# The first stage of a sparse-attention layer: norm, transposes and first projection in pairs of token tiles

## The chip, the cores and the metric

One Trainium2 chip, one of its cores. The metric is the device time of one execution of the whole program in microseconds (us); the kernel before ran three times, 481.62, 481.62 and 482.15 us, median 481.62.

The core's engines are named as in the profile: PE multiplies matrices into eight PSUM banks (PEld loads its weights), ACT is the scalar engine, DVE the vector engine, POOL the general engine; SP issues most DMA transfers. Each engine takes its instructions in the order in which they stand in its queue.

## The reference, cut to what matters

One layer of native sparse attention: x is 512 tokens x 1024, w_in has 5680 columns.

```
u = x * rsqrt(mean(x*x, -1) + 1e-6) * pre_norm_gain
q, kv, g, z = split(u @ w_in, [1024, 6*256, 48, 3072])
k_c, v_c, k_s, v_s, k_w, v_w = split(kv, 6)          # 4 groups x 64 each
kc = silu(blocks(k_c + k_pos) @ k_w1) @ k_w2          # 31 blocks of 32 tokens
vc = silu(blocks(v_c + v_pos) @ v_w1) @ v_w2
o  = three softmax branches (compressed, selected, window), each with a relative bias
y  = sum(sigmoid(g) * o * silu(z)) @ w_out
out = x + rms_norm(y) * post_norm_gain
```

## The kernel before

Every product is made of float32 numbers cut into a high part (a cast to fp32r) and a low part (what the cast left out), as three products, high*high, low*high and high*low, summed in one PSUM bank. The split of weights costs one cast and one subtraction for each piece of 128x1024 (four k-slices of 128 rows by 256 columns): even pieces go to ACT and POOL, odd pieces to DVE alone (L234 to L238). Weights come in through three raw buffers `wr`, split ones lie in three buffers `wh`/`wl`.

The first stage (L258 to L364) makes u transposed, that is `uh` and `ul` (high and low part, 1024 rows on partitions, 512 tokens across), and the first product from it, k_c (`p_kc`, two banks). Four token tiles `xs[t]` of 128x1024 come by DMA. `rms(t)` squares and sums one tile on ACT (L304) and raises the mean to -1/2 on POOL (L86, L90). `prep(t)` scales half a tile by the tokens' factor and by the norm weights, which two PE products with a row of ones had spread over 128 partitions in PSUM (L285 to L295, L314), transposes four 128x128 blocks into one PSUM bank (L319), and cuts the bank in two pieces of 128x256 into `uh` (ACT, L325) and `ul` (DVE, L326). The products k_c run over halves of 256 tokens (`hh`), k-slices, and two column halves (L354 to L362), with the transposes of tiles 2 and 3 in between. `tables()` (L328), written between the two halves, turns the bias table into two tensors with 20 PE products, most of 16 columns, reads them out on DVE, and writes them to DRAM, from where the softmax loads them back.

The second stage (L366 on) adds the position vectors to k_c (`blocks`, eight DVE additions of 64x496, L405), splits the sum into `bh`/`bl` (ACT, DVE and POOL, L414 and L415), makes v_c in the same way (`half_t(2,0)` and `half_t(3,1)`, 48 products of 512 columns, L245 to L247), then v, the MLPs over the blocks (L423 to L425), and so on. From there on the kernel keeps PE fed by a plan that the change doesn't touch.

The order of instructions on an engine comes from a scheduler that reorders what is written, within its own estimates; an instruction named in `keep_in_program_order` stays where it is written among its like. A tile pool that closes (a1, L258) gives its memory to the next one (a2): the first instruction that writes a tile of a2 waits for the last reader of what lay there.

Of the kernel before, what the change touches and what calls it, by code (L numbers as in the profile page):

```python
# [20 lines left out]
D = 1024  # L21
H = 16
DH = 64
G = 4
# [27 lines left out]
def nsa_layer(ctx: ExitStack, tc: tile.TileContext, x, pre_gain, post_gain, table, w_in, w_out,  # L52
# [204 lines left out]

    with tc.tile_pool(name="a1", bufs=1) as a1:  # L258
        grow = a1.tile([1, D], F32, name="grow")
        A.dma_start(grow, pre_gain)  # L260
        warm = a1.tile([1, 1], F32, name="warm")
        A.activation(warm, nhalf[0:1], AF.Tanh)
        one = a1.tile([1, 128], F32, name="one")
        V.memset(one, 1.0)
        ones = a1.tile([1, 128], F32R, name="ones")
        V.tensor_copy(ones, one)
        xs = []
        for t in range(NT):
            xt = a1.tile([128, D], F32, name="xt", bufs=4)
            SP.dma_start(xt, x[t * 128:(t + 1) * 128, :])  # L270
            xs.append(xt)
            if t == 1:
                load_ahead(1)
# [11 lines left out]
        gain = []  # L285
        gh = a1.tile([1, D], F32R, name="gh")
        gl = a1.tile([1, D], F32R, name="gl")
        for i in range(2):
            hs = slice(i * 512, (i + 1) * 512)
            V.tensor_copy(gh[:, hs], grow[:, hs])  # L290
            V.tensor_tensor(gl[:, hs], grow[:, hs], gh[:, hs].bitcast(F32), op=ALU.subtract)
            p = sb()
            T.matmul(p, ones, gh[:, hs], start=True, stop=False)
            T.matmul(p, ones, gl[:, hs], start=False, stop=True)
            gain.append(p)  # L295
        sq = a1.tile([128, D], F32, name="sq")
        banks = [tb, ob, tb]
        nb_ = 0

        rs_ = {}  # L300

        def rms(t):
            ss = a1.tile([128, 1], F32, name="ss", bufs=4)
            tc.keep_in_program_order(A.activation(sq, xs[t], AF.Square, scale=1.0 / 32, accum_out=ss))  # L304
            r = a1.tile([128, 1], F32, name="r", bufs=4)
            rstd(r, ss)
            rs_[t] = r

        def prep(t):
            nonlocal nb_  # L310
            r = rs_[t]
            for kq in range(2):
                hs = slice(kq * 512, (kq + 1) * 512)
                V.scalar_tensor_tensor(xs[t][:, hs], xs[t][:, hs], r, gain[kq], op0=ALU.mult, op1=ALU.mult)  # L314
                p = banks[nb_ % 3]()
                nb_ += 1
                for j in range(4):
                    k = kq * 4 + j
                    T.transpose(p[:, j * 128:(j + 1) * 128], xs[t][:, k * 128:(k + 1) * 128], ident)  # L319
                for jj in range(2):  # L320
                    i = kq * 2 + jj
# [650 lines left out]
```

## Time and profile before

| | |
|---|---|
| median of three runs | 481.62 us |
| the profiled execution | 481.59 us |
| its span (first to last instruction) | 479.80 us |
| PE / PEld / DVE / ACT / POOL busy | 95 / 78 / 68 / 57 / 37 % |
| first k_c product begins | 10.46 us |
| k_c done, v_c begins | 31.89 us |
| v_c done, v begins | 42.72 us |
| first softmax instruction on DVE begins | 116.9 us |

The span is what the trace shows; the 1.79 us between it and the execution's time lie around it. A row of the timeline gives start, length, engine, line and operands (out<-in), and in brackets the idle time of the engine before it with the instruction that ended it. Matmuls are pipelined: the length of one is longer than the distance to the next, and the distance is the cost.

### The profile page before, as it was taken

The numbers are of one execution on the slowest core, as the hardware profiler recorded it, in microseconds if no ns is written. First come the engines' busy times: TensorE is split into PE (matmuls) and PEld (weight loads), VectorE is DVE, ScalarE is ACT, GpSimd is POOL, SyncE is SP. The second block draws the span as 40 slices with busy tenths as digits, with TensorE's granted clock in tenths as the row PEclk, the third lists the DMA queues.
The fourth block names the chain that finished last, engine by engine and source line by source line (L and its number), as shares of the span: only waits on it lengthen the run. The fifth ranks groups of instructions, "written<-read, shape, count | busy, mean of one in ns | idle before, by whom it ended". The sixth has DMA issues, their size and how long they took to land.

```text
span 479.8 us, 6876 instructions
## 1 busy us (share of the span) xinstructions
PE 455.1 (95%) x2330; PEld 375.7 (78%) x2330; DVE 325.8 (68%) x788; ACT 273.6 (57%) x643; POOL 178.7 (37%) x139
## 2 busy tenths in 40 slices
PE   5999999999999989999999999998989999999993
PEld 3898788878888768878888778887768788877872
DVE  6779843844556898675689765668977456775486
ACT  5612232635647758765577865566677456657542
POOL 3324433334134253342243533423434325155153
PEclk9989999999999999999999999999999999999998
DMA  8498375461131231420221323213142121113104
GB/s 288 138 85 271 96 212 138 127 176 45 44 89 44 66 84 50 132 87 8 82 67 44 101 76 89 49 40 109 46 135 84 46 87 45 44 48 119 57 22 154
DMA packets 45501, 44.63 MB, mean 93 GB/s; under 512 B 7751, under 2 KB 38471, under 8 KB 45466
## 3 DMA queue, kind: packets, MB, share of 16 engines
q1 hardware_dynamic: 44424, 44.00, 32.4%
q8 instruction: 18, 0.29, 0.3%
q10 hardware_dynamic: 1042, 0.20, 0.2%
q14 instruction: 17, 0.14, 0.1%
HBM read 41.99 MB, written 2.20 MB: 92 GB/s over the span
## 4 chain that ended last, share of the span: by engine, by line
PE 79%; DVE 8%; ACT 7%; issue 2%; DMA 1%; POOL 1%; SPq 0%; DVEq 0%; ACTq 0%
PE ps_pj L146 9%; PE ps_pj L144 9%; PE ps_pj L145 9%; PE ps_s L589 7%; PE ps_t L683 6%; PE ps_o L692 4%; PE ps_o L691 3%; ACT p L602 2%; PE ps_pj L804 2%; PE ps_s L245 2%; PE ps_pj L806 2%; PE ps_pj L805 2%; PE ps_s L246 2%; PE ps_s L247 2%; PE ps_pj L246 2%
## 5 line engine op out<-in xcount | busy, mean ns | idle before, releaser
L116 POOL TENSOR_TENSOR wl<-wr,wh 128x1024 fp32r<-128x1024 f32 x47 | 113.7, 2418 | 160.7 <-ACT wh L113 146.0
L144 PE MATMUL ps_pj<-uh,wh 128*128 128x512 f32 x240 | 99.4, 414 | 0.0
L145 PE MATMUL ps_pj<-uh,wl 128*128 128x512 f32 x240 | 94.4, 393 | 0.0
L146 PE MATMUL ps_pj<-ul,wh 128*128 128x512 f32 x240 | 94.3, 393 | 0.0
L602 ACT ACTIVATE p<-p,nm 128x512 f32<-128x512 f32 (+3 forms) x128 | 71.7, 561 | 35.5 <-DVE nm L601 34.9
L113 ACT CAST wh<-wr 128x1024 fp32r<-128x1024 f32 x47 | 49.2, 1047 | 40.9 <-DMA wr<-in_nsa_w_in_dram 14.7
L687 DVE TENSOR_TENSOR ptl<-ps_t,pth 128x512 fp32r<-128x512 f32 x80 | 54.7, 686 | 22.5 <-ACT pth L686 21.9
L589 PE MATMUL ps_s<-kd,q 128*128 128x512 f32 (+5 forms) x256 | 62.2, 330 | 0.2 <-DVE zs L675 0.2
L686 ACT CAST pth<-ps_t 128x512 fp32r<-128x512 f32 x80 | 45.9, 578 | 21.7 <-PE ps_t L683 20.8
L146 PEld LDWEIGHTS ps_pj<-ul,wh 128*128 128x128 f32 x240 | 45.1, 188 | 9.9
L589 PEld LDWEIGHTS ps_s<-kd,q 128*128 128x128 f32 x256 | 45.2, 188 | 9.3 <-DVE zs L675 0.5
L601 DVE CUSTOM_DVE_ANT_0 p<-ps_s,bias 128x128 f32<-128x128 f32 (+3 forms) x80 | 34.7, 447 | 23.1 <-PE ps_s L589 22.6
L145 PEld LDWEIGHTS ps_pj<-uh,wl 128*128 128x128 f32 x240 | 45.3, 189 | 5.8
L144 PEld LDWEIGHTS ps_pj<-uh,wh 128*128 128x128 f32 x240 | 45.2, 188 | 5.3
L683 PE MATMUL ps_t<-ident,p 128*128 128x128 f32 x320 | 48.7, 272 | 0.0
L683 PEld LDWEIGHTS ps_t<-ident,p 128*128 128x128 f32 x320 | 39.1, 140 | 6.3
L691 PE MATMUL ps_o<-pth,vt 128*128 128x512 f32 x80 | 32.7, 409 | 2.7 <-ACT pth L686 1.4
L692 PE MATMUL ps_o<-ptl,vt 128*128 128x512 f32 x80 | 32.5, 407 | 0.8 <-DVE ptl L687 0.8
L703 POOL TENSOR_TENSOR y<-otmp,zs 128x256 f32<-128x256 f32 x16 | 11.8, 737 | 47.1 <-DVE otmp L700 47.0
L705 POOL TENSOR_TENSOR otmp<-otmp,zs 128x256 f32<-128x256 f32 x15 | 11.2, 748 | 45.9 <-DVE otmp L700 45.9
L699 DVE TENSOR_TENSOR otmp<-ps_o,otmp 64x256 f32<-64x256 f32 x32 | 13.2, 414 | 21.8 <-ACT otmp L698 21.3
L601 DVE CUSTOM_DVE_ANT_1 p<-ps_s,bias 128x256 f32<-128x256 f32 (+2 forms) x48 | 26.0, 550 | 2.1 <-PE ps_s L589 1.8
(260 smaller groups left out, 897.1 us busy)
## 6 DMA issues: line engine op xcount, KB each, us to landing
wr<-in_nsa_w_in_dram SPq DMA_DIRECT2D x36, 512.0 KB, 3.6
wr<-in_nsa_w_in_dram SPq DMA_DIRECT2D x16, 256.0 KB, 4.3
bias<-toepd SPq DMA_DIRECT2D x16, 256.0 KB, 6.5
wr<-in_nsa_w_out_dram SPq DMA_DIRECT2D x8, 512.0 KB, 4.6
xt<-in_x_dram SPq DMA_DIRECT2D x4, 512.0 KB, 4.1
wr<-in_nsa_cmp_k_w_dram SPq DMA_DIRECT2D x4, 512.0 KB, 4.9
wr<-in_nsa_cmp_v_w_dram SPq DMA_DIRECT2D x4, 512.0 KB, 3.7
xr<-in_x_dram SPq DMA_DIRECT2D x8, 256.0 KB, 2.8
```

Of the source, the lines that this page charges most:

```text
L113: A.copy(h[:, 0:kn], raw[:, 0:kn])
L116: el.tensor_tensor(l[:, 0:kn], raw[:, 0:kn], h[:, 0:kn].bitcast(F32), op=ALU.subtract)
L144: T.matmul(p, a, rh, start=k == 0, stop=False)
L145: T.matmul(p, b, rh, start=False, stop=False)
L146: T.matmul(p, a, rl, start=False, stop=k == KT - 1)
L589: T.matmul(po, qs[h][:, qt * 128:(qt + 1) * 128], kds[h // R][:, i, c0:c0 + n], start=i == 0, stop=i == 1)
L601: V.tensor_tensor_reduce(pd, src, bi, 1.0, BIG, ALU.add, ALU.min, st["nm"][:, hh:hh + 1])
L602: A.activation(po, po, AF.Exp, bias=st["nm"][:, hh:hh + 1], scale=-1.0, accum_out=st["rs"][:, hh:hh + 1])
L683: T.transpose(tp[:, hh * 128:(hh + 1) * 128], st["p"][hh][:, c:c + 128], ident)
L687: V.tensor_tensor(pl, tp, ph.bitcast(F32), op=ALU.subtract)
L691: T.matmul(acc, v, prev[1], start=j == 1, stop=False)
L692: T.matmul(acc, v, prev[2], start=False, stop=j == qt + 1)
```

## The change

Parts, in the order of the program:

- **Norm weights.** They are loaded as 8 rows of 128, transposed once on PE and copied to a [128, 8] tile (L316 to L318 of the changed kernel), so that one column holds the weights of a k-slice on partitions. The scaling by them moves behind the transpose: ACT multiplies while it casts `uh`, DVE multiplies and subtracts in one instruction for `ul`. What is left in front of the transpose is the tokens' factor alone, SBUF to SBUF (`norm`).
- **Squares.** Half of each tile's sum of squares is made on ACT, half on DVE (`rms`).
- **Pairs.** `prep(pair, k)` transposes the blocks of one k-slice of two token tiles into a bank of its own (two transposes, 256 columns used), five banks in turn.
- **Weights.** The two pieces of k_c's weights are split in eight parts of 128x256, all by ACT and POOL (`piece`); the third piece is requested before the small loads.
- **Order.** All this is written down instruction by instruction with `O`, which keeps it in program order; `after()` makes what follows be issued after it. k_c runs pair by pair, k-slice by k-slice.
- **Tables.** `tables()` and the position vectors move behind the first half of v_c; the eight additions of k_c stay in front of them. The splits of `blk` move into the second pool.

```diff
-        for i in range(2):
-            V.tensor_copy(gh[:, hs], grow[:, hs])
-            V.tensor_tensor(gl[:, hs], grow[:, hs], gh[:, hs].bitcast(F32), op=ALU.subtract)
-            T.matmul(p, ones, gh[:, hs], start=True, stop=False)
-            T.matmul(p, ones, gl[:, hs], start=False, stop=True)
...
+        p = sb()
+        O(T.transpose(p[:, :KT], grow, ident[:KT, :KT]))
+        gain = a1.tile([128, KT], F32, name="gain")
+        O(V.tensor_copy(gain, p[:, :KT]))
+        banks = [tb, ob, tb, sb, sb]
...
+        def rms(t):
+            O(A.activation(sq[:, 0:512], xs[t][:, 0:512], AF.Square, scale=1.0 / 32, accum_out=ss[:, 0:1]))
+            O(V.tensor_tensor_reduce(sq[:, 512:D], xs[t][:, 512:D], xs[t][:, 512:D], 1.0 / D, 0.0,
+                                     ALU.mult, ALU.add, ss[:, 1:2]))
+            rstd(r, ss[:, 0:1], ss[:, 1:2])
...
+        def norm(t, i):
+            hs = slice(i * 512, (i + 1) * 512)
+            O(V.tensor_scalar(xs[t][:, hs], xs[t][:, hs], rs_[t], None, op0=ALU.mult))
+
+        def prep(pair, k):
+            p = banks[nb_ % 5]()
+            for e in range(2):
+                O(T.transpose(p[:, e * 128:(e + 1) * 128], xs[pair * 2 + e][:, k * 128:(k + 1) * 128], ident))
+            dh = uh[k // 2][:, k % 2, pair * 256:(pair + 1) * 256]
+            dl = ul[k // 2][:, k % 2, pair * 256:(pair + 1) * 256]
+            O(A.mul(dh, p[:, 0:256], gain[:, k:k + 1]))
+            O(V.scalar_tensor_tensor(dl, p[:, 0:256], gain[:, k:k + 1], dh.bitcast(F32), op0=ALU.mult, op1=ALU.subtract))
...
+        def piece(i, k):
+            h, l = tiles[i]
+            O(A.copy(h[:, k], raws[i][:, k]))
+            O(P.tensor_tensor(l[:, k], raws[i][:, k], h[:, k].bitcast(F32), op=ALU.subtract))
...
+        for k in range(8):
+            kc(0, k)
+            if k in (1, 3):
+                rms(2 + k // 2)
+            if k < 6:
+                piece((k + 2) // 4, (k + 2) % 4)
+            if k < 5:
+                prep(0, k + 3)
+            elif k == 5:
+                norm(2, 0)
+                norm(3, 0)
+                prep(1, 0)
...
+        with after():
+            split_ahead(2)
+        for k in range(8):
+            if k < 6:
+                prep(1, k + 2)
+            kc(1, k)
+        with after():
+            kpt = load_pos("k")
+            vpt = load_pos("v")
+        kblk = blk_add(p_kc, kpt)
+        with after():
+            split_ahead(4)
+        p_vc = [sb(), sb()]
+        half_t(2, 0, p_vc)
+        with after():
+            tables()
```

Three places show how instructions move. POOL at the start, before (`wl`, 128x1024, is a split; `r` the tokens' factor; `bl` the split of the k_c blocks):

```order
L86 TENSOR_SCALAR r<-ss 128x1
L90 TENSOR_TENSOR r<-r,nhalf 128x1
L86 TENSOR_SCALAR r<-ss 128x1
L90 TENSOR_TENSOR r<-r,nhalf 128x1
L116 TENSOR_TENSOR wl<-wr,wh 128x1024
L86 TENSOR_SCALAR r<-ss 128x1
L90 TENSOR_TENSOR r<-r,nhalf 128x1
L86 TENSOR_SCALAR r<-ss 128x1
L90 TENSOR_TENSOR r<-r,nhalf 128x1
L116 TENSOR_TENSOR wl<-wr,wh 128x1024
L463 MEMSET vx 64x512
```

and now, where L382 is a split of one eighth:

```order
L88 TENSOR_SCALAR r<-ss 128x1
L90 TENSOR_TENSOR r<-r,nhalf 128x1
L88 TENSOR_SCALAR r<-ss 128x1
L90 TENSOR_TENSOR r<-r,nhalf 128x1
L382 TENSOR_TENSOR wl<-wr,wh 128x256 x3
L88 TENSOR_SCALAR r<-ss 128x1
L90 TENSOR_TENSOR r<-r,nhalf 128x1
L382 TENSOR_TENSOR wl<-wr,wh 128x256 x2
L88 TENSOR_SCALAR r<-ss 128x1
L90 TENSOR_TENSOR r<-r,nhalf 128x1
L382 TENSOR_TENSOR wl<-wr,wh 128x256 x3
L116 TENSOR_TENSOR wl<-wr,wh 128x1024 x2
```

The first two pieces were one subtraction on POOL and one on DVE; now POOL has eight, and the two later factors stand between them.

DVE from k_c's end on, before (`blk` is k_c with positions, `ptk` the positions; the table part, `nth` to `cb`, stood well ahead of these rows):

```order
L388 COPY ptk<-ps_t 128x32
L388 COPY ptv<-ps_t 128x32
L405 TENSOR_TENSOR blk<-ps_pj,ptk 64x16x31 x8
L115 CAST wh<-wr 128x1024
L116 TENSOR_TENSOR wl<-wr,wh 128x1024
L415 TENSOR_TENSOR bl<-blk,bh 128x496 x2
L405 TENSOR_TENSOR blk<-ps_s,ptv 64x16x31 x8
```

and now, with the end of the fourth weight piece's split (the first L116) ahead of them:

```order
L350 TENSOR_SCALAR ntab<-tabx 32x16
L351 MEMSET ntab 1x16
L116 TENSOR_TENSOR wl<-wr,wh 128x1024
L266 COPY ptk<-ps_t 128x32
L266 COPY ptv<-ps_t 128x32
L274 TENSOR_TENSOR blk<-ps_pj,ptk 64x16x31 x8
L354 CAST nth<-ntab 33x16
L115 CAST wh<-wr 128x1024
L355 TENSOR_TENSOR ntl<-ntab,nth 33x16
L447 CAST kw2h<-w2k 128x2x64
L116 TENSOR_TENSOR wl<-wr,wh 128x1024
L364 COPY toep<-ps_t 16x512
```

The table's `nth` and `ntl`, for which PE's table products wait, stand behind the eight additions, and `toep`, the read-out that frees the PSUM bank of the later ones, behind one more split.

PE, the table products before, in the middle of k_c:

```order
L246 MATMUL ps_pj<-uh_83,wl 128x256
L247 MATMUL ps_pj<-ul_87,wh 128x256
L342 MATMUL ps_s<-hsr,nth 16x512
L319 MATMUL ps_t<-ident,xt 128x128 x4
L343 MATMUL ps_s<-hsr,ntl 16x512
L342 MATMUL ps_s<-hsr,nth 16x128
L343 MATMUL ps_s<-hsr,ntl 16x128
L349 MATMUL ps_s<-nth,hcr 128x16
L350 MATMUL ps_s<-ntl,hcr 128x16
```

and now, in the second half of v_c (512-column products into ps_s):

```order
L362 MATMUL ps_t<-hsr,nth 16x512
L362 MATMUL ps_t<-hsr,nth 16x128
L247 MATMUL ps_s<-ul_86,wh 128x512
L363 MATMUL ps_t<-hsr,ntl 16x512
L363 MATMUL ps_t<-hsr,ntl 16x128
L245 MATMUL ps_s<-uh_82,wh 128x512
L246 MATMUL ps_s<-uh_82,wl 128x512
L247 MATMUL ps_s<-ul_86,wh 128x512
L245 MATMUL ps_s<-uh_82,wh 128x512
L246 MATMUL ps_s<-uh_82,wl 128x512
L247 MATMUL ps_s<-ul_86,wh 128x512
L245 MATMUL ps_s<-uh_83,wh 128x512
```

The sixteen products of 16 columns (L369, L370) follow on the last of these rows; eleven products of v_c come after them.

## Rows read from the trace of the kernel before

**Rows 1.** The page's busy row.

```profile
PE 455.1 (95%) x2330; PEld 375.7 (78%) x2330; DVE 325.8 (68%) x788; ACT 273.6 (57%) x643; POOL 178.7 (37%) x139
```

**Rows 2.** Timeline: start us, us, instruction; where v_c begins and where it ends.

```profile
31.89 0.50 PE L245 MATMUL ps_s<-uh,wh 128*128 128x512 f32 x1
...
42.72 0.19 PEld L478 LDWEIGHTS ps_pj<-wh,uh 128*128 128x128 f32 x1
```

**Rows 3.** Windows of core 0: length; busy us by engine; PEclk, DMA share, GB/s.

```profile
10.40:14.70 4.30, 3.80 (x16) 3.50 (x17) 2.64 (x7) 1.91 (x6) 1.03 (x1) 1.00 0.55 116
20.40:24.80 4.40, 4.40 (x34) 3.62 (x34) 3.24 (x9) 2.06 (x6) 2.77 (x2) 1.00 0.09 11
24.80:28.20 3.40, 3.40 (x19) 3.40 (x18) 1.41 (x7) 0.37 (x1) 0.11 (x1) 0.51 1.11 224
...
43.00:80.00 37.00, 36.07 (x189) 30.79 (x188) 23.48 (x27) 11.35 (x16) 15.28 (x7) 1.00 0.55 168
```

**Rows 4.** Timeline, PE: neighbours at the low and at the high clock.

```profile
13.79 0.41 PE L246 MATMUL ps_pj<-uh,wl 128*128 128x256 f32 x1
14.00 0.41 PE L247 MATMUL ps_pj<-ul,wh 128*128 128x256 f32 x1
...
14.87 0.28 PE L246 MATMUL ps_pj<-uh,wl 128*128 128x256 f32 x1
14.99 0.28 PE L245 MATMUL ps_pj<-uh,wh 128*128 128x256 f32 x1
...
18.21 0.63 PE L319 MATMUL ps_o<-ident,xt 128*128 128x128 f32 x4 [0.19 <-issue]
18.60 0.36 PE L247 MATMUL ps_pj<-ul,wh 128*128 128x256 f32 x1
```

**Rows 5.** Timeline up to the first k_c product, with [idle before <-releaser].

```profile
5.36 1.06 ACT L304 ACTIVATE sq<-xt 128x1024 f32<-128x1024 f32 x1 [0.20 <-DMA xt<-in_x_dram]
7.95 1.05 ACT L113 CAST wh<-wr 128x1024 fp32r<-128x1024 f32 x1 [1.44 <-DMA wr<-in_nsa_w_in_dram]
10.46 0.58 PE L245 MATMUL ps_pj<-uh,wh 128*128 128x256 f32 x1 [0.68 <-ACT uh L325]
```

**Rows 6.** Groups by line, 0 to 43 us: busy us, mean ns | idle.

```profile
L325 ACT CAST uh<-ps_t 128x256 fp32r<-128x256 f32 x10 | 3.5, 375 | 2.9 <-PE ps_t L319 2.2 <-DVE ul L326 0.7
L326 DVE TENSOR_TENSOR ul<-ps_t,uh 128x256 fp32r<-128x256 f32 x10 | 4.0, 414 | 3.9 <-ACT uh L325 3.9
L405 DVE TENSOR_TENSOR blk<-ps_pj,ptk 64x496 f32<-64x496 f32 x8 | 5.4, 673 | 0.1
L116 POOL TENSOR_TENSOR wl<-wr,wh 128x1024 fp32r<-128x1024 f32 x3 | 7.1, 2375 | 11.1 <-ACT wh L113 11.1
L90 POOL TENSOR_TENSOR r<-r,nhalf 128x1 f32<-128x1 f32 x4 | 2.5, 619 | 0.3
```

**Rows 7.** The page's group of 256-column products on POOL.

```profile
L703 POOL TENSOR_TENSOR y<-otmp,zs 128x256 f32<-128x256 f32 x16 | 11.8, 737 | 47.1 <-DVE otmp L700 47.0
```

**Rows 8.** Timeline: DVE's split alone and beside POOL, and PE's wait.

```profile
38.48 1.23 DVE L116 TENSOR_TENSOR wl<-wr,wh 128x1024 fp32r<-128x1024 f32 x1
...
52.61 2.83 POOL L116 TENSOR_TENSOR wl<-wr,wh 128x1024 fp32r<-128x1024 f32 x1
53.11 3.41 DVE L116 TENSOR_TENSOR wl<-wr,wh 128x1024 fp32r<-128x1024 f32 x1
...
56.57 0.38 PE L425 MATMUL ps_t<-wl,bh 128*124 128x256 f32 x1 [0.93 <-DVE wl L116]
```

**Rows 9.** Timeline, PE and POOL: table products, and who waits for them.

```profile
21.89 0.25 PE L349 MATMUL ps_s<-nth,hcr 33*128 33x16 f32 x1
22.00 0.25 PE L350 MATMUL ps_s<-ntl,hcr 33*128 33x16 f32 x1
...
24.39 0.52 POOL L463 MEMSET vx<- 64x512 f32 x1 [1.04 <-PE ps_s L350]
```

**Rows 10.** Line L601, the softmax on DVE: duration, first and last start.

```profile
L601 DVE CUSTOM_DVE_ANT_0 p<-ps_s,bias x80: 278/423/694, 116.9 to 412.5; 128x128 f32<-128x128 f32 x32, 128x512 f32<-128x512 f32 x16, 128x384 f32<-128x384 f32 x16, 128x256 f32<-128x256 f32 x16
```

More of the change, by code (lines that the diff above doesn't have):

```diff
@@ L256, in half_t, with load_pos, blk_add, O @@
                       k == 0, k == KT - 1)
-    with tc.tile_pool(name="a1", bufs=1) as a1:
-        grow = a1.tile([1, D], F32, name="grow")
-        A.dma_start(grow, pre_gain)
+    nb = G * NCMP
+    def load_pos(nm):
+        pr = small[nm, "p"]
+        V.tensor_copy(pr[:, 1], pr[:, 0])
+        p = tb()
+        T.transpose(p[:, :32], pr.rearrange("p a b -> p (a b)"), ident[:32, :32])
+        pt = sm.tile([128, 32], F32, name="pt" + nm)
+        V.tensor_copy(pt, p[:, :32])
+        return pt
+    def blk_add(banks, pt):
+        blk = keep.tile([128, 16, G, NCMP], F32, name="blk", tag="kd", bufs=4)
+        for m, p in enumerate(banks):
+            for gp in range(2):
+                for lp in range(2):
+                    V.tensor_tensor(
+                        blk[lp * 64:lp * 64 + 64, :, 2 * m + gp, :],
+                        view(p[gp * 64:gp * 64 + 64, :], lp, [[2, 16], [16, NCMP]]),
+                        view(pt[gp * 64:gp * 64 + 64, :], lp, [[2, 16], [0, NCMP]]), op=ALU.add)
+        return blk
+    with tc.tile_pool(name="a1", bufs=1) as a1:
+        last = {}
+        def O(ins):
+            tc.keep_in_program_order(ins)
+            last[ins.ins.engine] = ins.ins
+        def after():
+            es = ExitStack()
+            for ins in last.values():
+                es.enter_context(tc.issue_after(ins))
+            return es
+        grow = a1.tile([KT, 128], F32, name="grow")
+        A.dma_start(grow, dview(pre_gain, 0, [[128, KT], [1, 128]]))
         warm = a1.tile([1, 1], F32, name="warm")
         A.activation(warm, nhalf[0:1], AF.Tanh)
[L263 to L266, printed above, removed]
         xs = []
@@ L346, in tables @@
             cb = sm.tile([128, G, 8, R], F32, name="cb")
-            p = sb()
+            p = tb()
             for j in range(8):
@@ L379, in nsa_layer @@
-    with tc.tile_pool(name="a2", bufs=1) as a2:
-        nb = G * NCMP
-        def load_pos(nm):
-            pr = small[nm, "p"]
-            V.tensor_copy(pr[:, 1], pr[:, 0])
-            p = tb()
-            T.transpose(p[:, :32], pr.rearrange("p a b -> p (a b)"), ident[:32, :32])
-            pt = sm.tile([128, 32], F32, name="pt" + nm)
-            V.tensor_copy(pt, p[:, :32])
-            return pt
+        norm(0, 0)
+        norm(1, 0)
+        norm(0, 1)
+        norm(1, 1)
+        piece(0, 0)
```

98 lines of the change are left out of this document (32 added, 66 removed).

## The prediction

> **What bounds the kernel now.** I read the page's busy row first: PE is busy for 95% of the span [rows 1], so the other engines count only where PE waits for them. Second I read the timeline of the first 43 us, which is all that the change touches: v_c begins at 31.89 and is done at 42.72 [rows 2], which makes 10.83 us for 48 products, 0.2256 us each. Up to there I ask when PE begins, how long it works and where it waits; behind it I ask only whether a later wait moves, because PE's list is the same from there on.
>
> Third the clock. The windows show the granted clock at 0.51 from 24.8 to 28.2, the lower level (1.2 GHz), behind a stretch of 16-column table products, transposes and gaps [rows 3]. Until about 14.6 PE ran at that level too: its 256-column products start 0.21 us apart there and 0.12 apart right after [rows 4], although the window from 10.4 to 14.7 prints 1.00.
>
> **The start.** The first k_c product begins at 10.46, behind ACT's `uh`; ACT had the first weights at 7.95, after waiting 1.44 us for their DMA [rows 5]. The same two x tiles still go ahead of those weights on SP, so 7.95 stays. The tokens' factors are off this path: x tile 1 lands by 5.36 [rows 5]; half a square (about 0.6 of the 1.06), its read-out (0.2), two POOL steps (0.3 and 0.62 [rows 6]), one half-tile of `norm` (0.4) and the transposes of slice 0 end near 8.0. `norm` on 512 columns isn't in the trace: at most 0.74 (the old scaling from PSUM had about that), at least 0.35; both are covered by the weights' landing. So ACT casts an eighth (0.35, a share of 1.05) and writes `uh` with the weight multiplied in (0.375 as the old cast [rows 6], bounds 0.33 to 0.6): first product at 8.7, the second, behind POOL's first piece, at 9.2. The start gains 1.7 us.
>
> **k_c.** Work on PE: 96 products and 32 transposes, 6 of them before 8.7. I let the clock rise at 14.6 as before. From 9.2 to 14.6 there are 25 slots of 0.213: 19 more products and 6 transposes. Left are 76 products of 0.12 and 20 transposes of 0.0975 (four in 0.39 [rows 4]), 9.1 + 1.95 = 11.1 us, so 25.7 if nothing waits. ACT (0.35 + 0.375 a slice) and DVE (0.41 for `ul` [rows 6]) keep under the 0.92 us of a slice. POOL doesn't quite: a piece of 256 columns costs 0.74, taken from the page's POOL products of that width [rows 7]; its bounds are 0.6, a quarter of the whole split [rows 6], and 0.87 (0.74 stretched as 2.83 to 2.375 beside DVE [rows 6, 8]). Three pieces end at 10.9. Then comes the factor of tile 2, for which ACT squares only behind `uh` of slice 3 (11.9) and DVE behind its `ul`; it ends at 13.2. Two pieces end at 14.7; the factor of tile 3 waits for squares behind slice 5's `uh` and ends at 16.6; the sixth piece at 17.4. PE wants that one at 16.3: a wait of 1.1 us. k_c is done at 25.7 + 1.1 = 26.8, where before it was 31.9. The norm weights cost nothing extra on PE (one transpose, early, instead of four products).
>
> **v_c with the tables in it.** The 5 us aren't kept, because the tables left k_c. They cost 16 products at 0.11 [rows 9] and four wide ones, 0.6 together: 2.4 us, now between v_c's. And they wait. `nth` stands behind eight additions of 0.673 [rows 6]. DVE's last `ul` ends about 1.3 us ahead of k_c's end, two slices early; then come the fourth weight piece (1.23 [rows 8] and a cast of 0.7) and a handful of small copies, so the additions begin 1.8 behind k_c's end and `nth` is there at 26.8 + 1.8 + 5.4 + 0.2 = 34.2. PE is through 29 products of v_c at 26.8 + 0.2 + 29 x 0.2256 = 33.5: it waits 0.75. For `ntl` (behind another cast) 0.35, for the PSUM bank that `toep` frees (behind a split of 1.23 [rows 8] and a 0.67 read-out) 0.2. Behind each wait PE holds v_c's remaining products. End: 26.8 + 0.2 + 10.83 + 2.4 + 1.3 = 41.5. My handovers of about 0.05 us each are lean; over so many I add 0.35: 41.9, against 42.72. Gain 0.85 us.
>
> Casts to `bh` and POOL's `vx` must wait for the last table product, whose memory the second pool takes over. That wait is old for `vx` (1.04 us behind L350 [rows 9]); for `bh` it is new. Behind it ACT holds the load of the gate weights and the cast of the seventh weight piece, POOL the `bl` halves and the same piece. `bl` for the first MLP ends near 44 and is wanted 5.4 us behind v_c's end, near 47; nothing waits. SP sends the tables and the bias loads some 12 us later than before; the softmax wants them at 116.9 [rows 10].
>
> **One wait behind.** At 56.57 PE waits 0.93 us for DVE's split of the second MLP piece, which took 3.41 us beside POOL's 2.83 where it takes 1.23 alone [rows 8]; it is part of the 0.93 us that PE lacks between 43 and 80 [rows 3]. In the new order that split stands one `bl` (1.73 contended) earlier, but v_c's additions begin about 0.6 later behind v_c's end, and `wgs` (0.55) stands before it: net 0.6 earlier. So 0.6 of the 0.93 go; the bounds are 0.93 and -1.
>
> Sum: 0.85 + 0.6 = 1.45 us off a span of 479.80, 478.35; with the 1.79 around it 480.14. The profiled execution (481.59) and the median (481.62) agree within 0.03. I predict **480.1 us**.
>
> **A rule on the clock.** From 10.4 to 14.7 PE was at work for most of the time and still at the low level; what it had done until 10.46 were transposes and the four products of the norm weights [rows 3 to 5]. The Trainium skill, "TensorE: Matmul & The Clock Gate", Part 4 (PE-mode transpose), says that transposes don't count as busy for the clock as products do. The trace agrees, without proving it. By it the clock follows the products and the time is that of the second case below (479.3), without it that of the sum (480.1).
>
> **A rule on POOL.** DVE's split with two SBUF inputs grows from 1.23 to 3.41 beside POOL [rows 8]. The Trainium skill, "GPSIMD Engine Reference", section Specifications, says that POOL shares its SBUF access with DVE instructions that have two SBUF inputs or run in the two-port mode; the trace agrees for the first kind. By it the squares and `norm` on DVE and the eight pieces on POOL would stretch each other, which is the third case (481.4); without it the sum stands.
>
> **The ways it can go.**
> - *As summed*: 480.1, alone 479.3 to 480.9 (waits on POOL 0.3 less to 0.4 more, the later wait between 0.93 gone and 0.2 grown). 42%.
> - *The clock rises earlier.* The first product is now 1.7 us earlier, and no break follows it as before, when PE stopped again for `wl` and `ul`. If the clock rises midway between the first product and 14.6, near 11.6, 3 us of slots at 0.213 would cost 0.12: 14 x 0.093 = 1.3 us less, of which PE gives back some 0.5 because POOL's pieces don't come faster. 479.3. 23%.
> - *DVE and POOL hold each other up in the first pair.* Both squares (0.65 each) stretched by 2.8 as in the split beside POOL [rows 8] cost 1.15 us each; the first hides at the low clock, the second lies on the path to POOL's factor and so to the sixth piece; a little more comes from `norm`. Gain 1.45 - 1.3 = 0.15: 481.4, no change. For it speaks the 3.41; against it that POOL is idle during most of them, waiting for their results. Or the written order does no more than the scheduler's did, with the same outcome. 22%.
> - *Slower: the table products starve v_c.* If DVE's split of the fourth weight piece runs beside POOL's split of the fifth, it takes 3.41 for 1.23, and the additions, `nth` and PE's wait move 2.2 us: PE idles over 3 us in and around the table products. Behind such a stretch the clock fell before [rows 3]; 3.4 us at the low level lose half, 1.6. 480.1 + 2.2 + 1.6 = 483.9. It decides from a split of about 2.5 us on; less is a matter of the first case. Against it: POOL's starts only when k_c ends, DVE's before. 13%.
>
> **How the numbers follow.** About 0.2% (1 us) is what a measurement here tells from no change. Faster by more: four fifths of the first case, nearly all of the second, a sixth of the third: 0.60. Slower by more: the last, 0.13. Within: 0.27. The range reaches from a good outcome of the second case (478.8) to the third with some more contention (481.7).
>
> **What will show it.** In the changed profile: the first k_c product near 8.7 and still behind the weights' DMA; PE's one gap in k_c near 16 to 17.5, released by POOL's L382; v_c beginning near 27; gaps at L362 and L363 released by DVE; v beginning near 41.9 with the clock at 1.00 throughout v_c; the wait at the second MLP piece 0.3 or less. Wrong would be: gaps in k_c ended by ACT's or DVE's `uh`/`ul`; a clock of 0.5 in v_c; PE waiting at the first MLP; or v beginning a microsecond and more earlier and the end not, which would say that a later wait takes the gain.

## The result: 483.2 us, slower by 0.56%, and the profile after

The changed kernel takes 483.23 us, the median of 20 runs (481.84 to 484.57); the kernel before took 480.64 beside it (20 runs, 478.61 to 482.69). The ratio is 1.0056, 95% interval 1.0042 to 1.007: about 2.7 us slower, where 1.45 us faster was forecast. The profiled execution of the changed kernel has a span of 482.3 us (479.80 before); its mean granted clock, 0.988, is the lowest among the 20 runs, and six of them have it.

The page's busy row hardly moves [rows 1]:

```profile
PE 454.7 (94%) x2327; PEld 375.1 (78%) x2327; DVE 325.6 (68%) x789; ACT 275.5 (57%) x650; POOL 182.9 (38%) x146
```

Where the time went is read from the timeline of the first 47 us. PE, k_c's start and the change from the first pair of token tiles to the second (start us, us, instruction, [idle before <-releaser]):

```profile
8.12 0.48 PE L342 MATMUL ps_t<-ident,xt 128*128 128x128 f32 x1 [0.86 <-DVE xt L335]
9.16 0.58 PE L393 MATMUL ps_pj<-uh,wh 128*128 128x256 f32 x1
...
14.92 0.39 PE L394 MATMUL ps_pj<-uh,wl 128*128 128x256 f32 x1 [0.70 <-POOL wl L382]
...
17.98 0.38 PE L394 MATMUL ps_pj<-uh,wl 128*128 128x256 f32 x1 [0.92 <-POOL wl L382]
...
18.56 0.28 PE L395 MATMUL ps_pj<-ul,wh 128*128 128x256 f32 x1
18.96 0.33 PE L342 MATMUL ps_s<-ident,xt 128*128 128x128 f32 x1
19.82 0.43 PE L342 MATMUL ps_s<-ident,xt 128*128 128x128 f32 x1 [0.54 <-DVE xt L335]
19.91 0.56 PE L393 MATMUL ps_pj<-uh,wh 128*128 128x256 f32 x1
20.27 0.41 PE L394 MATMUL ps_pj<-uh,wl 128*128 128x256 f32 x1
```

The first k_c product starts 1.3 us earlier than before [rows 5]. Then PE waits twice for POOL's pieces and, from 18.68 to 19.82, for DVE's `norm` of tiles 2 and 3; after that its products are 0.21 us apart, as at the low clock [rows 4]. What held the `norm` up stands beside it, on POOL and DVE:

```profile
17.21 2.28 POOL L382 TENSOR_TENSOR wl<-wr,wh 128x256 fp32r<-128x256 f32 x3
...
17.89 1.88 DVE L335 TENSOR_SCALAR xt<-xt,r 128x512 f32<-128x512 f32 x2
...
21.20 0.87 DVE L335 TENSOR_SCALAR xt<-xt,r 128x512 f32<-128x512 f32 x2
```

A pair of such scalings takes 1.88 us beside POOL's pieces and 0.87 when POOL is idle. The windows (length; busy us by engine; PEclk, DMA share, GB/s) show the price [rows 3]. The first row is of the kernel before, the others are of the changed kernel:

```profile
14.70:20.40 5.70, 5.51 (x46) 5.21 (x45) 4.93 (x16) 4.60 (x9) 1.87 (x4) 1.00 0.75 246
...
14.70:20.40 5.70, 3.91 (x25) 3.31 (x26) 4.18 (x7) 2.46 (x8) 3.97 (x7) 0.96 0.32 92
20.40:24.80 4.40, 4.40 (x28) 4.40 (x27) 2.24 (x5) 2.51 (x5) 1.32 (x1) 0.67 0.40 123
...
43.00:80.00 37.00, 37.00 (x182) 31.30 (x181) 24.90 (x27) 12.07 (x19) 19.24 (x10) 0.95 0.76 175
```

PE worked 3.91 of 5.70 us (5.51 before), and behind that the granted clock was at the lower level (1.2 GHz) until about 23.3. From 43 to 80 PE never waits (36.07 of 37 before), as forecast, but the clock falls once more, behind the table products (PE's timeline):

```profile
30.55 0.50 PE L245 MATMUL ps_s<-uh,wh 128*128 128x512 f32 x1
...
42.18 0.25 PE L370 MATMUL ps_t<-ntl,hcr 33*128 33x16 f32 x1
...
43.88 0.63 PE L246 MATMUL ps_s<-uh,wl 128*128 128x512 f32 x1
44.31 0.63 PE L247 MATMUL ps_s<-ul,wh 128*128 128x512 f32 x1
...
46.01 0.63 PE L518 MATMUL ps_pj<-wh,uh 128*128 128x512 f32 x1
```

v_c begins at 30.55 and v at 46.01; before these were 31.89 and 42.72 [rows 2]. So 1.3 us earlier has become 3.3 later; the later wait that goes takes 0.93 off.

**The same order in other executions.** Four kernels of the experiments (e3_spread, e7_no_small, e12_one_wide, e15_bias_alone) have the changed kernel's order on every engine through k_c. In none of their profiles does the clock fall at the change of pairs, although PE's wait can be just as long. Two rows of e12_one_wide (PE busy 3.95 of 5.70 us from 14.70 to 20.40), then v_c's and v's beginning in e15_bias_alone:

```profile
19.97 0.33 PE L342 MATMUL ps_s<-ident,xt 128*128 128x128 f32 x1 [0.54 <-DVE xt L335]
20.40:24.80 4.40, 4.40 (x41) 4.40 (x39) 2.85 (x7) 3.15 (x6) 2.04 (x1) 1.00 0.41 123
...
28.34 0.50 PE L251 MATMUL ps_s<-uh,wh 128*128 128x512 f32 x1
...
43.98 0.63 PE L523 MATMUL ps_pj<-wh,uh 128*128 128x512 f32 x1
```

In these four v_c begins at 28.34 to 29.55, in the changed kernel's profile at 30.55. The fall at the change of pairs belongs to that execution. What two profiles differ by, one execution each, can be the clock alone.

**A second way to read the runs.** Every run lists its span and PE's mean granted clock. (1 - clock) x span estimates what the low level cost it, as if PE had work all the time: 5.8 us in the changed kernel's profile (0.012 x 482.3). The start is not in it, where the products are 0.21 us apart and the window prints 1.00 all the same. The mean over the changed kernel's 20 runs is 4.2, over 101 runs of the kernel before 3.1. What is left of the mean time is 479.0 and 478.0 (standard errors 0.2 and 0.1). By this split the clock is about half of the 2.2 us between the means, and waits and extra work are the other half. The runs themselves say that half is too much: among the 101, one us more of the estimate goes with 0.66 us more of time, among the changed kernel's 20 with 0.32. The table uses the split (for the changed kernel against the 101 runs, for the others against the runs of before on the same chip); the standard errors are 0.3 to 0.7 in both of its columns. Three executions of 753 to 1587 us (one of e9_stacked, two of the kernel before) are left out.

| kernel | ratio to before, 95% | lost to the clock | the rest, against before beside it |
|---|---|---|---|
| changed | 1.0056 (1.0042, 1.007) | 4.2 | +1.0 |
| e1_norm_act | 1.0022 (1.000, 1.0043) | 3.9 | +0.5 |
| e2_fill | 1.0036 (1.0017, 1.0054) | 3.0 | +1.7 |
| e3_spread | 1.0264 (1.0239, 1.0289) | 11.1 | +4.6 |
| e4_tables_back | 1.0262 (1.0235, 1.0289) | 8.8 | +6.9 |
| e10_pieces | 0.9996 (0.9976, 1.0017) | 2.9 | +0.4 |
| e5_norm_pieces | 1.0005 (0.9989, 1.002) | 2.8 | +0.4 |
| e8_groups | 1.0076 (1.0051, 1.01) | 3.0 | +3.7 |
| e7_no_small | 1.0063 (1.004, 1.0085) | 3.6 | +2.5 |
| e12_one_wide | 1.0014 (0.9993, 1.0036) | 3.5 | +0.5 |
| e6_move_alone | 1.0078 (1.0047, 1.0108) | 3.9 | +3.0 |
| e11_move_clean | 1.0049 (1.0028, 1.0071) | 3.9 | +2.0 |
| e9_stacked | 0.9974 (0.9954, 0.9993) | 3.5 | -1.7 |
| e13_best | 0.9955 (0.9938, 0.9973) | 2.9 | -2.1 |
| e14_bias_late | 1.0015 (0.999, 1.0041) | 3.8 | -0.5 |
| e15_bias_alone | 1.0033 (1.0012, 1.0054) | 4.5 | 0.0 |

### The profile page after: what moved, and what is told of

The parts are those of the page before. It is cut to its first block, busy times and chain, and to the rows that moved or that the text cites. A ratio compares the mean times of both kernels' runs of the same rounds, so it can differ in the third digit from the quotient of the medians.

```text
span 482.3 us, 6878 instructions
## 1 busy us (share of the span) xinstructions
PE 454.7 (94%) x2327; PEld 375.1 (78%) x2327; DVE 325.6 (68%) x789; ACT 275.5 (57%) x650; POOL 182.9 (38%) x146
## 4 chain that ended last, share of the span: by engine, by line
PE 79%; DVE 8%; ACT 7%; issue 2%; POOL 1%; DMA 1%; DVEq 0%; SPq 0%; POOLq 0%; ACTq 0%
PE ps_pj L146 9%; PE ps_pj L144 9%; PE ps_pj L145 9%; PE ps_s L629 7%; PE ps_t L723 6%; PE ps_o L732 4%; PE ps_o L731 3%; ACT p L642 2%; PE ps_s L245 2%; PE ps_s L247 2%; PE ps_s L246 2%; PE ps_pj L844 2%; PE ps_pj L846 2%; PE ps_pj L845 2%; PE ps_s L714 1%
## 5 line engine op out<-in xcount | busy, mean ns | idle before, releaser
L116 POOL TENSOR_TENSOR wl<-wr,wh 128x1024 fp32r<-128x1024 f32 x46 | 111.9, 2432 | 155.9 <-ACT wh L113 141.3
L113 ACT CAST wh<-wr 128x1024 fp32r<-128x1024 f32 x46 | 48.2, 1047 | 34.0 <-DMA wr<-in_nsa_w_in_dram 12.1
```

What stands on the lines that cost most here:

```text
L113: A.copy(h[:, 0:kn], raw[:, 0:kn])
L116: el.tensor_tensor(l[:, 0:kn], raw[:, 0:kn], h[:, 0:kn].bitcast(F32), op=ALU.subtract)
```

## The experiments

**The change of pairs: norm on ACT.**

```diff
-            O(V.tensor_scalar(xs[t][:, hs], xs[t][:, hs], rs_[t], None, op0=ALU.mult))
+            if t < 2: O(V.tensor_scalar(...))      # as before
+            else:     O(A.mul(xs[t][:, hs], xs[t][:, hs], rs_[t]))
```

> Only edit to the changed kernel: the four scalings (norm) of token tiles 2 and 3 go from DVE to ACT, in the same places of the order. In the changed kernel they took 0.94 us each on DVE beside POOL's pieces (0.43 once POOL was idle), PE waited 0.32 and 0.54 us for them at 18.96 and 19.82, and the granted clock was 0.5 from 19.9 to 23.3. Theory A (the wait for DVE at the pair change, and the lower clock behind it): ACT needs about 0.6 for one, so PE's two waits shrink to 0.3 together, k_c ends 0.6 earlier by the waits alone and 2.0 to 2.5 us earlier if the clock then stays at 1.00: 481.0 to 482.7. Rival B (the order by pairs itself costs: transposes stand between products whatever they wait for): the waits shrink but the clock falls all the same, and the time stays within 0.6 of the changed kernel's 483.2.

481.99 us, inside theory A's range; the interval of its ratio just meets the changed kernel's. The window that read 0.67 is at the high level:

```profile
20.40:24.80 4.40, 4.39 (x39) 4.19 (x37) 1.99 (x5) 3.46 (x7) 2.38 (x1) 1.00 0.36 117
```

But so it is in the four profiles above, where `norm` is still on DVE. v_c begins at 28.25 and v at 44.22, against 28.34 and 43.98 in e15_bias_alone, and the clock's second fall is still behind the table products. What `norm` on ACT is worth by itself isn't shown.

**The same gap, filled.**

```diff
         def prep(pair, k, fill=0):
+            for _ in range(fill):      # 3 ahead of prep(1, 0), 6 ahead of prep(1, 1)
+                O(T.matmul(p[:, 256:512], tiles[0][0][:, 0, 0:128], uh[0][:, 0, 0:256], start=True, stop=True))
```

> Only edit to the changed kernel: nine extra 256-column products, whose results nobody reads, stand where PE waits at the pair change, three before the first transposes of pair 1 and six before the second. The waits for DVE stay; PE works in them. Theory A, its clock part (PE's idle time at the pair change brings the granted clock to 0.5 for 3.4 us, which costs 1.6): the clock stays at 1.00, and the time falls by 1.2 to 1.6 us to about 481.7 to 482.0. Rival B (the clock falls because transposes stand between the products, or for a reason earlier in the stage): the fall stays, and the time is unchanged or up to 0.5 worse, 483.2 to 483.7.

482.76 us, above theory A's range. In the profile `norm` is as late as before and PE's second wait stays, but the clock does not fall. That alone shows nothing, since it does not fall in the four profiles without the filling either; over the runs the time lost to the clock is 3.0 for 4.2 (difference 1.2, standard error 0.45), which speaks for theory A.

```profile
20.09 0.33 PE L344 MATMUL ps_s<-ident,xt 128*128 128x128 f32 x1 [0.53 <-DVE xt L335]
20.17 0.36 PE L395 MATMUL ps_pj<-uh,wh 128*128 128x256 f32 x1
20.38 0.28 PE L396 MATMUL ps_pj<-uh,wl 128*128 128x256 f32 x1
```

The size was missed: the second group of six (0.7 us) ran where there was nothing left to wait for, and the rest is 0.7 larger than the changed kernel's. Rival B, the fall by the transposes themselves, is out: with the same transposes between the products the clock stays up here and in the four profiles.

**POOL's order.** The pieces go ahead of the factors, alone and together with the norm on ACT.

```diff
-            if k in (1, 3):
-                rms(2 + k // 2)
             if k < 6:
                 piece((k + 2) // 4, (k + 2) % 4)
+            if k in (0, 2):
+                rms(2 + k // 2)
```

> The changed kernel with two edits: norm of token tiles 2 and 3 on ACT (as in the run that gave 481.99), and on POOL the weights' pieces ahead of the factors: in each slice the piece stands before the squares of a tile, and these come one slice earlier. In the changed kernel PE waited 0.70 at 14.92 and 0.92 at 17.98 for pieces that stood on POOL behind a factor that itself waited for squares. Theory A (the new order puts short waits for POOL and DVE where PE has no other work): both waits go, k_c ends 1.2 to 1.6 earlier than with norm on ACT alone (28.1), and the time is 480.4 to 480.9. Rival B (ACT can't cast and scale any faster, the waits only change their name): PE waits 1 us or more for uh on ACT, and the time stays at 481.5 to 482.2.

> The changed kernel with the pieces ahead of the factors on POOL and the squares one slice earlier; norm stays on DVE. It tells what this edit is worth without norm on ACT. Theory A (PE's waits for pieces, 1.6 us, and for norm beside POOL, with the clock's fall behind them, are one knot: earlier pieces leave POOL free when norm runs, so that norm takes 0.45 instead of 0.94): both waits shrink, no fall at the pair change, and the time is 480.5 to 481.3. Rival (the two add up): only the waits on POOL go, 1.1 us, the fall at the pair change stays, 482.0 to 482.4.

480.86 and 481.38 us: both as fast as the kernel before, and the two don't add up. The pieces' order alone recovers what the change lost, with `norm` still on DVE: the interval of its ratio is clear of the changed kernel's, 0.6% lower. The same edit is worth 0.2% between e1_norm_act and e5_norm_pieces and 0.2% between e15_bias_alone and e14_bias_late, where the intervals overlap; so its size, some 1 to 3 us, is known only roughly. PE's timeline of e10_pieces:

```profile
16.42 0.39 PE L394 MATMUL ps_pj<-uh,wl 128*128 128x256 f32 x1 [0.54 <-POOL wl L382]
...
18.26 0.33 PE L342 MATMUL ps_s<-ident,xt 128*128 128x128 f32 x1 [0.54 <-DVE xt L335]
...
27.43 0.50 PE L245 MATMUL ps_s<-uh,wh 128*128 128x512 f32 x1
...
41.87 0.39 PE L518 MATMUL ps_pj<-wh,uh 128*128 128x512 f32 x1
```

v_c begins at 27.43 and v at 41.87: the prediction had 27.0 and 41.9. The wait for `norm` is as long as in the changed kernel (1.14 us from the last product to the second pair of transposes in both), so theory A's reason (POOL free when `norm` runs) is wrong: the two scalings still run beside pieces and take 1.50 us. Against the changed kernel's profile v_c begins 3.1 us earlier: about 0.9 by shorter waits for POOL, 1.7 by the clock's fall that is missing, 0.2 by the start, and 0.5 because the clock rose at 11.6 in this execution and at 13.1 in that one. Only the 0.9 can be put down to the edit from the profiles; over the runs the time lost to the clock is 2.9 for 4.2 (standard error of the difference 0.6).

**The tables.** e4_tables_back puts `tables()` between the two pairs again, e3_spread puts one small product behind each of v_c's, e8_groups makes two groups of eight (with POOL's order and the norm of e5_norm_pieces).

> Only edit to the changed kernel: the tables go back between the two pairs of k_c, where they stood before; all else stays. Theory A: the lower clock at the pair change stays, because the table products wait for DVE there, but the second fall in v_c is gone and v_c takes 10.9 us: the time falls by 1 to 2 us, to 481.2 to 482.2. Rival C (the move of the tables alone makes the difference to the kernel before): the early start then shows fully and the time is 479.0 to 480.0, below the kernel before. Rival B (the first stage's order costs and the tables don't matter): 483.0 or more.

493.57 us: all theories missed. The tables' operands wait where nothing else can run, 1.41 us for `hsr` behind a weight cast on ACT, 1.43 for `ntl` on DVE, 0.74 for the read-out, and the clock falls behind it (0.63 from 25 to 30, 0.74 from 30 to 36); waits of 2.3 and 1.9 for splits follow. With the new order of the first stage the old place is no longer open. The change of pairs stands ahead of all this, with the same wait for `norm` (0.54), and the clock stays at 1.00 behind it.

> Only edit to the changed kernel: the sixteen 16-column table products don't stand in a row inside v_c, but one behind each of the first sixteen products of v_c's second half (their operands were moved to memory that lives longer, so that the order can be written). Theory A, its second clock part (a block of sixteen 16-column products of 0.11 us each brings the clock to 0.5 from 43.8 to 47.2): no fall there, 1.6 us less, 481.3 to 481.9. Rival (the fall follows the small products wherever they stand, or has another cause): still 0.5 for 3.4 us somewhere from 43 to 50, and the time within 0.4 of the changed kernel's 483.2.

493.65 us: wrong by 12. Some of v's products had moved ahead of v_c's second half as well. PE's timeline:

```profile
38.57 0.49 PE L506 MATMUL ps_s<-uh,wl 128*128 128x512 f32 x1
38.99 0.27 PE L375 MATMUL ps_t<-ntl,q 33*128 33x16 f32 x1
39.20 0.49 PE L506 MATMUL ps_s<-ul,wh 128*128 128x512 f32 x1
...
43.75 0.79 PE L506 MATMUL ps_s<-ul,wh 128*128 128x512 f32 x1
44.47 0.38 PE L373 MATMUL ps_t<-nth,q 33*128 33x16 f32 x1
44.78 0.79 PE L506 MATMUL ps_s<-uh,wh 128*128 128x512 f32 x1
```

A wide and a small product together take 0.63 us where 0.23 + 0.11 = 0.34 stood in the sum: each change between 128 and 33 rows costs some 0.15. PE counts as busy all the time, and yet the clock is low from 41.7 to 55.3.

> As the kernel with norm on ACT and pieces ahead of the factors, and the sixteen small table products in two groups of eight, with fourteen of v_c's products between the groups (operands in longer-lived memory). One behind each wide product cost 0.63 us a pair for 0.34 in the run before and held the clock at 0.5 for 13 us; a group costs one change from 128 to 33 rows and back, some 0.3 us. Theory A (a group of eight, 0.9 us, is too short to bring the clock down): no fall, 1.6 us less and 0.3 more than with the one block, 479.1 to 479.6. Rival (the small products bring the clock down in any grouping): falls of 3.4 us or more remain, 480.7 or more.

484.53 us (ratio 1.0076, 1.0051 to 1.01). The clock stays at 1.00 in v_c here, but thirteen of v's products had moved ahead of it, and PE waits 2.5 us for splits later. Missed.

**The block itself.** e7_no_small keeps two of the sixteen small products; e12_one_wide has one of 128 columns in their place.

> The changed kernel without fourteen of the sixteen 16-column table products (the compressed part's bias table is filled from the first eighth alone, so that part of its computation is left out). They start 0.11 us apart in the changed kernel, 1.56 us for fourteen. Theory A (the block of small products brings the clock to 0.5 behind it): the fall at 43.8 is gone, and the time is 1.56 + 1.6 less, 480.0 to 480.4. Rival (the fall has another cause, such as v_c's products between waits): only the 1.56 go, 481.5 to 481.9.

> The changed kernel with one 128-column product in place of the sixteen 16-column ones (the compressed part's bias table holds no meaningful values then, so that part of its computation is left out), and with DVE's order kept, which the run without the small products had changed: there the second MLP piece's split came behind other work and PE waited 1.6 and 1.7 us for splits later. Theory A (the block costs 1.7 us of PE and a fall of the clock of 1.6, and nothing takes it back): 480.0 to 480.6. Rival (the splits behind v_c bound the time, so that what v_c gains comes back as PE's waits for wl): 482 or more, with waits of 2 us or more between 43 and 80.

483.56 and 482.21 us. Without fourteen products v begins at 42.42, 3.6 us earlier than in the changed kernel's profile and 1.6 earlier than in e15_bias_alone, and nothing is won (waits, PE: us in total, times, longest):

```profile
PE ps_pj L519 <- POOL wl L116: 1.7, 1, 1.7
PE ps_t L467 <- DVE wl L116: 1.6, 1, 1.6
```

The edit had moved small copies on DVE, and with them the second MLP piece's split. With DVE's order kept (e12_one_wide) one wait of 1.3 is left, and of some 3 us expected 1.0 arrives by the medians, 2.0 by the ratios. Both theories were half right: without the block v_c takes 12.9 and 12.8 us where it took 15.5, and part of what v_c gains comes back as a wait for a low part.

**The move alone** (of the tables, with the position vectors and the splits of `blk` that go with them), in the kernel before: first with v_c's early products inside k_c, then with these held back.

```diff
-            if hh == 0:
-                tables()
...
+        with after():
+            half_t(2, 0, p_vc)          # e6_move_alone: without this `with`
+        with after():
+            tables()
```

> The kernel before with one part of the change alone: the tables stand behind the last k_c product, inside v_c, as in the changed kernel; the first stage (four transposes of one token tile at a time, whole weight splits, norm weights by products, the order of loads) stays as it was. Theory A (the tables bring one fall of the clock wherever they stand and cost some 0.5 us more among wide products): k_c ends 4.5 earlier and v_c takes 5 to 5.5 us longer, so that the time is 480.6 to 482.0. Rival C (the move alone makes the changed kernel slower): 482.8 or more. Rival D (the move is a gain that the first stage's order gives away): 480.0 or less.

> The kernel before with the tables moved into v_c alone, as in the run that gave 484.74, but with v_c's products held behind k_c's (there two of them stood inside k_c and PE waited 0.68 and 0.89 us around them). Theory A (the move itself costs little: one fall of the clock either way, some 0.5 us more for changes between 33 and 128 rows): 480.8 to 482.0. Rival C (moving the tables behind k_c is the costly part of the change: v_c, the casts to bh that wait for the last table product and the splits behind them come late): 483 or more.

484.74 us (1.0078, 1.0047 to 1.0108) and 483.94: rival C in both. Moving the tables is by itself a loss of about 2.4 us in the old first stage. In e11_move_clean v begins at 43.14 (42.72 before), and a new wait stands behind it, 0.3 longer than the old one of 0.93, which is gone:

```profile
58.77 0.50 PE L507 MATMUL ps_pj<-wl,uh 128*128 128x512 f32 x1 [1.27 <-POOL wl L116]
```

The two make up 0.8 of the 2.2 us between the spans of the two profiles (482.0 and 479.8); where the rest of the loss lies isn't shown.

**A version that beats both.** High and low part of the table stand on different rows of one operand, so that one product does the work of two; POOL's order and the norm are those of e5_norm_pieces.

```diff
-                T.matmul(p[:, j * H:(j + 1) * H], hcr[:, j * 128:(j + 1) * 128], nth, start=True, stop=False)
-                T.matmul(p[:, j * H:(j + 1) * H], hcr[:, j * 128:(j + 1) * 128], ntl, start=False, stop=True)
+                T.matmul(p[:, j * H:(j + 1) * H], hcr[:, j * 128:(j + 1) * 128], nth, start=True, stop=True)
...          # nth: high part on rows 0-32, low part on 64-96; hcr: the one-hot rows on both
```

> The kernel with norm of tiles 2 and 3 on ACT and the pieces ahead of the factors (480.86, as fast as the kernel before), and the tables in half as many products: the high and the low part of the table stand on rows 0 to 32 and 64 to 96 of one operand, the one-hot matrix on both, so that one product adds both parts. Eight 16-column products go (0.11 us each, 0.9 us) and two wide ones (0.3), and one change between 33 and 128 rows (some 0.3). Theory A (the tables' time in v_c is on PE's path and the block behind which the clock falls is now half as long): 1.2 to 1.5 us less by PE's time and no fall of the clock behind the block, 478.9 to 479.6. Rival (what v_c gains is given back at the weights' splits behind it, as 3.3 us were in the run without the small products): PE waits 1 us or more for wl between 43 and 80 us, and the time is 480.4 or more.

479.93 us, ratio 0.9974 (0.9954 to 0.9993), 0.3 above theory A's range and below the rival's. v begins at 40.38, 1.9 us earlier than in e5_norm_pieces; the wait that the rival named is 0.2.

**SP's queue.** Where e10_pieces waits 0.87 us at 64.0, ACT had waited 9.54 for a weight piece (timeline of POOL, SP, ACT and PE):

```profile
43.46 2.40 POOL L116 TENSOR_TENSOR wl<-wr,wh 128x1024 fp32r<-128x1024 f32 x1
46.33 4.63 SPq L166 DMA_DIRECT2D cbs<-cmpb  x4
...
52.74 0.39 SPq L103 DMA_DIRECT2D wr<-in_nsa_cmp_k_w_dram  x1
...
60.43 1.05 ACT L113 CAST wh<-wr 128x1024 fp32r<-128x1024 f32 x1 [9.54 <-DMA wr<-in_nsa_w_in_dram]
...
63.98 0.50 PE L520 MATMUL ps_pj<-wl,uh 128*128 128x512 f32 x1 [0.87 <-POOL wl L116]
```

The buffer of the next weights is free when POOL ends at 45.86, and their DMA goes out at 52.74, behind the tables' loads; the piece that ACT waits for follows it. Three kernels send `load_bias(0)` behind two more weight pieces: e14_bias_late is e10_pieces with this edit, e15_bias_alone the changed kernel, e13_best e9_stacked; only SP's order differs.

```diff
-            load_bias(0)        # in tables()
+            if kp == 2:         # in the v and MLP loop, in written order on SP
+                load_bias(0)
```

> The changed kernel with the pieces ahead of the factors (481.38, 0.9996 of the kernel before), and on SP the loads of the first bias tables behind the next two weight pieces instead of ahead of them; no other engine's order changes. Theory (SP's queue): the next weights' DMA goes out near 46 instead of 52.7, ACT's cast comes 4 us earlier, PE's wait of 0.87 at 64.0 is gone, and the time is 0.8 to 1 less, 480.3 to 480.7, ratio near 0.998. Rival (bandwidth or buffers bound the weights): the wait stays within 0.3 of 0.87, the ratio within 0.001 of 0.9996.

> The changed kernel with only SP's order changed: the first bias tables' loads behind the next two weight pieces. Theory (in the changed kernel PE comes so late to these weights that SP's queue costs nothing: no wait between 43 and 80): no change, ratio to the kernel before 1.004 to 1.007. Rival (the queue is part of the changed kernel's loss): 1 us less, ratio 1.003 or less.

> The kernel with norm of tiles 2 and 3 on ACT, pieces ahead of the factors and the tables in half as many products (479.93), and on SP the loads of the first bias tables behind the next two weight pieces instead of ahead of them. Theory (SP's queue: the moved table loads hold up the weights): the wait for a low part between 60 and 65 goes (0.2 there), little else moves, 479.0 to 479.9. Rival (the weights are bound by DMA bandwidth or by buffers, not by the queue): the wait stays or grows to 1 us, 480 to 481.

481.58, 482.40 and 479.42 us. The wait is gone in all three (PE busy 20.00 of 20 us from 60 to 80), and e13_best is the fastest kernel of this study. But e14_bias_late isn't faster than e10_pieces and missed its range: its rest is about 0.9 lower against the kernel before beside it (standard error 0.4), as the theory says, and it lost more to the clock (3.8 for 2.9). e15_bias_alone came out near where the rival put it, though the changed kernel's profile shows no wait that it could remove. In time the queue's price isn't settled; in the traces it is a wait of under 1 us that shows as soon as v_c ends early.

## Why the prediction was wrong

The step that failed is PE's path from 14.6 to the end of v_c. The sum had one wait for POOL ahead of v_c (1.1 us), none at the change of pairs, and the high clock throughout. In the changed kernel's profile the waits for POOL are 1.9 us, the one for `norm` is 1.0, and two falls of the clock cost 1.7 each. Over the runs the order on POOL, factors ahead of pieces, costs 1 to 3 us (e10_pieces and two more pairs of kernels); how much of that is waits and how much low clock stays open. The items follow the changed kernel's profile.

- **The start: direction right, 0.46 short.** The weights did land first (ACT's cast at 7.58), but they were not the cover: `norm` of tile 1 came behind POOL's factor (7.54) and took some 0.55 us, and PE's transposes waited for it at 8.12. "Both are covered by the weights' landing" failed.
- **POOL's wait in k_c: place right, too small.** 1.1 us at the sixth piece was forecast; PE idles 0.92 at the sixth, and 0.70 come at the fourth, behind tile 2's factor, which the sum had ending in time.
- **The change of pairs: missed.** The sum has no wait there. `norm` was priced for the first pair only, and the case "DVE and POOL hold each other up" counted the squares and called POOL "idle during most of them". In the trace it is the `norm` of tiles 2 and 3 that meets three pieces on POOL: 0.94 us each for 0.43, and PE idles 1 us. The rule of the Trainium skill, "GPSIMD Engine Reference", section Specifications, that was cited there names DVE instructions in the two-port mode besides those with two SBUF inputs; `norm` has one, and it stretched; whether it runs in that mode no run here shows.
- **The clock: put at nothing.** From 14.6 on every term was worked out at the high level; the sum took the fall of the kernel before out with the tables and put none in. In the changed kernel's profile the clock fell behind the change of pairs (1.7 us) and behind the table products (1.1 before v begins, 0.6 after). The first fall stands in this profile alone among those with the same order; the second stands in five of the seven with the block of sixteen where the change has it (also in e1_norm_act, e2_fill, e14_bias_late and e15_bias_alone, not in e5_norm_pieces and e10_pieces).
- **The clock's rise.** It came early (products 0.12 apart from 13.1, between the sum's 14.6 and the second case's 11.6), worth 0.7. The first product stood at 9.16, and at 10.46 in the kernel before, with transposes ahead of both. That would fit the rule cited from the Trainium skill, "TensorE: Matmul & The Clock Gate", Part 4 (PE-mode transpose). But the time of the rise isn't bound to the products: e6_move_alone and e11_move_clean have the old start, and the first of them is at the high level behind two products, with nothing but transposes ahead of them from 7.10 on; the second is only at 16.6. So one trace that agrees was luck. Rows of e6_move_alone, PE:

```profile
10.39 0.47 PE L245 MATMUL ps_pj<-uh,wh 128*128 128x256 f32 x1 [0.46 <-ACT uh L359]
11.22 0.39 PE L246 MATMUL ps_pj<-uh,wl 128*128 128x256 f32 x1 [0.36 <-POOL wl L116]
11.44 0.28 PE L245 MATMUL ps_pj<-uh,wh 128*128 128x256 f32 x1
11.56 0.28 PE L246 MATMUL ps_pj<-uh,wl 128*128 128x256 f32 x1
```

- **The sum for v_c's beginning:** 27.0 + 0.46 (start) + 0.8 (POOL: with the gaps around its waits 1.9 for 1.1) + 1.0 (`norm`) + 1.7 - 0.7 (clock) + 0.3 (slices of 0.935 us for 0.915) = 30.6; it began at 30.55.
- **v_c with the tables: right without the clock.** 15.46 us less 1.1 is 14.4, forecast 14.9; the waits for `nth`, `ntl` and the bank were smaller than the 1.3 summed. (`uh` with the weight multiplied in took 0.47 us, within its bounds; ACT was never late.)
- **The later wait: right.** The 0.93 us at the second MLP piece are gone (0.6 forecast).
- **The slower case: near in number, not in kind.** Its 483.9 came close to 483.2, but what it rests on didn't happen: DVE's split of the fourth weight piece took 1.22 us at 30.28, and PE didn't idle at the table products.
- **SP's queue: a term left out.** "The softmax wants them at 116.9" asks when the moved loads are needed, not what they are put in front of. In the changed kernel that cost no wait; in e10_pieces it does, as e14_bias_late shows, and in e12_one_wide and e11_move_clean a wait stands behind the same row of loads, where it wasn't tested.

That e10_pieces comes so near the forecast of the stage (27.43 and 41.87 for 27.0 and 41.9) is in part luck: the wait for `norm`, about 1 us, is still missing in the sum, and a clock that rose at 11.6 instead of 14.6 makes up for it (1.3 us by the prediction's second case). e14_bias_late, with the same order on PE, has 28.00 and 43.96, with a fall behind the table products. e10_pieces shows too why 480.1 would not have come even then: its gain of 0.85 at v_c's end was measured against a trace whose clock had fallen in the tables, and over the runs both kernels lose about as much to the clock (2.9 and 3.1). In the rest e10_pieces is 0.4 behind the kernel before (standard error 0.3).

## What to carry to other kernels

When a stage is rewritten so that PE starts earlier, look for the places where it then has one thing to do and three engines to wait for: waits of some 3 us in all were followed in one execution by a fall of the clock that cost 1.7 more. Work out each stage's sum at both clock levels, and compare kernels by their runs' mean clock as well as by their times, since one trace may have a fall more or less. Before a fall in one trace is called the cause, look at other executions with the same order on the engines. For every DMA that is moved, ask what stands behind it on its queue.

## What the runs showed that I had not expected

- The clock falls behind the same gap in one execution and not in another. All kernels here wait about 2.2 us for DVE between 349 and 364 us, and in 8 of the 17 profiles the clock falls behind it. In e10_pieces (first window row; length, PE busy, PEclk, DMA share, GB/s) it does, in e5_norm_pieces (second fence) it does not, and the 1.7 us is as large as most differences between these kernels.

```profile
354.00:357.00 3.00, 3.00 (x11) 0.60 0.90 280
```

```profile
354.00:357.00 3.00, 3.00 (x15) 1.00 0.86 282
```

- The sixteen 16-column products in a row took 0.11 us each. Behind them the clock fell in the profiles of the changed kernel, e1_norm_act, e2_fill, e14_bias_late and e15_bias_alone; in e10_pieces, which has the same order on PE as e14_bias_late, it did not.
- Between products on 128 rows and on 33 rows PE loses some 0.15 us per change (0.63 for 0.34 in e3_spread), though the trace shows it as busy.
- A scaling on DVE with one input from SBUF takes 0.43 us alone and 0.94 beside POOL's 256-column subtractions (0.75 in e10_pieces, where POOL works beside it for part of the time).
